# Moving the split activations to the right end of on-chip memory, and starting every large tile at a multiple of 64 bytes

## The chip, the core and the metric

The kernel runs on one NeuronCore of a Trainium2 chip. TensorE (PE) does the matrix products, VectorE (DVE), ScalarE (ACT) and GpSimd (POOL) the elementwise work, SyncE (SP) issues most transfers. All of them work on SBUF, a memory of 128 partitions; a tile is a range of byte addresses that is the same in every partition, and this case is about these addresses. The metric is the device time of one execution in microseconds (us), the median of several runs: 1369.34 us before the change.

## What is computed

Two transformer blocks on 256 tokens of 1024 features, all in fp32. The first has a projection, two attentions, gates and a MLP; the second has a gated mixing branch, a dilated attention, and PEER, a layer that picks 16 of 16384 experts per head:

```
h2 = rms_norm(x);  x = x + rms_norm(square(relu(h2 @ w_up)) @ w_down)
...
e, g = top-16 of the scores of xb @ w_query       # per token and head
act = gelu(sum_d xb[t,d] * expert_u[e,d])         # (t, h, k)
out = sum (g * act)[t,h,k] * expert_v[e,:]
```

The kernel does PEER densely: it multiplies the tokens by all of `expert_u` (16384 x 1024), weighs the result by a table that is zero but for the chosen experts, and multiplies by all of `expert_v`. These two products are 128 MB of weights and most of the time.

## The kernel before, in words

**Three products for one.** Each fp32 operand is split into a high and a low part of the type fp32r (`h` and `l`), and `mm3` (L164 to L167) issues three matmuls: high by high, high by low, low by high. Weights come by DMA into a `raw` tile of 128 x 1024 (4096 bytes per partition); ACT copies the high part to `wh` (L115), DVE or POOL subtracts to get `wl` (L121). The split activations are the tiles `hh` and `hl` (8192 bytes each: two token blocks, eight slices of 128 x 128), made by `parts()`.

**Which operand moves.** In `matmul(p, x, y)` the operand `x` is loaded into the array ahead of the matmul (a LDWEIGHTS of 128 columns, in the row PEld of the profile), and `y` streams through it. In `stations` (gate, w_up, w_query, expert_u) a weight slice is loaded and the activations stream, 256 columns in two runs of 512 bytes; in the trace these are `mid<-hh,wh`, `mid<-hl,wh`, `mid<-hh,wl`. In `project`, `rows_product`, `down` and `v_units` an activation slice is loaded and 512 columns of weights stream (`acc<-wh,ah` and the like).

**Stages and slots.** The order of all instructions on every engine is fixed when the program is built. The weights go round through slots: four pairs of the pool `ring` (always), four of the pool `wkx` (from the branch products until the routing), and in the MLP two more of the pool `wkm`, which lies on the right side. In the MLP the slots take turns as wkx, ring, wkx, ring, wkx, ring, wkx, ring, wkm, wkm; a `w_up` unit and a `w_down` unit, which alternate, take two slots each. So one w_up unit runs its first 24 matmuls on a wkx slot and its next 24 on a ring slot, and every fifth unit lies on the two wkm slots.

**Expert stages.** `expert_u` is 64 units of 48 matmuls, all on ring slots, with the activations `hh`, `hl` of the pool `hp`. During the first 32 units DVE does the routing (top-16 searches) beside the splits. During the last 32 it builds the table: for each token two tiles `m` (L1019, L1020), which PE multiplies (four matmuls `acc<-m,m` per pair of tokens, between each 12 matmuls of expert_u), then multiplies the result into `acts`. `expert_v` is 64 units of 24 matmuls of 512 columns: ring slots stream over the split `acts`, tiles `ah` and `al`.

**Addresses.** A pool takes its place when it is opened, at the left end of what is free, or at the right end where it is opened with `side="right"`; each of its tiles follows the one before it. `hp` is opened after `const`, `ring` and `small`, and so lies just right of them. The begin of the tiles that matter (bytes in a partition; every slice of 128 columns is 512 bytes, so all slices of a tile share the remainder):

| tile | begin before | mod 64 | mod 256 | begin after | mod 64 | mod 256 |
|---|---|---|---|---|---|---|
| ring: wh (first of 4) | 36128 | 32 | 32 | 37888 | 0 | 0 |
| ring: wl (first of 4) | 52512 | 32 | 32 | 54272 | 0 | 0 |
| hp: hh, hl | 70176, 78368 | 32 | 32 | 212928, 221120 | 0 | 192 |
| wkx: wh, wl (first) | 123008, 139392 | 0 | 128 | 107136, 123520 | 0 | 128 |
| MLP hh, hl (right side) | 161760, 169952 | 32 | 224 | 145344, 153536 | 0 | 192 |
| MLP wkm: wh (first of 2) | 206816 | 32 | 224 | 190400 | 0 | 192 |
| MLP mfh (first of 5) | 186336 | 32 | 224 | 169920 | 0 | 192 |
| expert_v: ah, al (first) | 152096, 156192 | 32 | 32 | 136192, 140288 | 0 | 0 |

Of the kernel before, what the change touches and what calls it, by code (L numbers as in the profile page):

```python
# [9 lines left out]
F32 = mybir.dt.float32  # L10
# [9 lines left out]
P = 128  # L20
# [10 lines left out]
HALF = 32  # L31
WBUFS = 4
RBUFS = 4


C_CAUS = 0
# [3 lines left out]
C_I50 = C_FREQ + 24  # L40
# [35 lines left out]
def block_kernel(ctx: ExitStack, tc: tile.TileContext, a, out, dbg=None):  # L76
    nc = tc.nc
    vec, act, pe, pool = nc.vector, nc.scalar, nc.tensor, nc.gpsimd

    const = ctx.enter_context(tc.tile_pool(name="const", bufs=1))  # L80
    ring = ctx.enter_context(tc.tile_pool(name="ring", bufs=1))
    small = ctx.enter_context(tc.tile_pool(name="small", bufs=4))
    hp = ctx.enter_context(tc.tile_pool(name="hp", bufs=1))
    ps = ctx.enter_context(tc.tile_pool(name="ps", bufs=1, space=PSUM))
    dram = ctx.enter_context(tc.tile_pool(name="dram", bufs=1, space=DRAM))
    xres = dram.tile([P, TB, D], F32, name="xres")
# [6 lines left out]

    cycle, raws, last_split = [ring] * WBUFS, [ring] * RBUFS, [None]
    count, turn_raw = [0, 0], [0]
# [151 lines left out]
    def project(*args, **kw):  # L247
        for _ in projecting(*args, **kw):
            pass
# [155 lines left out]
    xp = p1.enter_context(tc.tile_pool(name="xp", bufs=1))  # L405
# [78 lines left out]

    whole = [(1024, 1024)] * 2
    project(hh, hl, KB, [(f"w_in_n{W1_BLOCKS[0][0]}", 0, [(768, 768)] * 2, 384, emit_cq)])
    cst = xp.tile([P, C_I50], F32, name="cst")
    nc.sync.dma_start(out=cst, in_=a["consts"][:, :C_I50])
    tok = const.tile([P, C_N - C_I50], F32, name="tok")
    pool.dma_start(out=tok, in_=a["consts"][:, C_I50:])  # L490
    i50, i128 = tok[:, :NCAND], tok[:, NCAND:]
# [460 lines left out]
    cycle[:] = [ring] * WBUFS  # L952
    raws[:] = [ring] * RBUFS
    b1.close()
# [211 lines left out]
```

## Time and profile before

| | us |
|---|---|
| median of three runs | 1369.34 (1367.41 to 1370.09) |
| the profiled execution | 1366.17 |
| its span in the trace | 1364.4 |
| PE busy | 1320.8 (97%) |
| DVE busy | 982.0 (72%) |
| ACT busy | 667.1 (49%) |
| mean granted clock of TensorE | 0.993 of full speed |

The trace records when each instruction ran. Matmuls are pipelined, so the duration of one (0.28 us for 256 columns) overlaps the next; what one costs is the distance from its start to the start of the next. It is read here from the chain of waits (time of a stretch over its count of matmuls) or from the timeline (first and last start of a run of equal matmuls). The granted clock is 1.00 (the 2.4 GHz level) in all stretches that are compared.

### The profile page before, as it was taken

To read this page: it belongs to the slowest core of one execution; us is meant where nothing else is said; L and a number is where in the kernel's file an instruction comes from. 1 tells how busy PE (TensorE), PEld (TensorE's weight loads), DVE (VectorE), ACT (ScalarE), POOL (GpSimd) and SP (SyncE) were. 2 spreads that over 40 slices of the span, in tenths; PEclk is the share of its full clock that TensorE was granted. 3 is DMA by queue.
4 is the path that set the end of the run, shared out by engine and by line. 5 is a ranking of instruction groups with operands and counts; after the bars stand their busy time and mean duration, and the time that the engine had idled before them with its cause. 6 is when DMAs were issued, how large, how long until landed. Compare 5 with 4: busy or idle time off the path is not lost.

```text
span 1364.4 us, 22115 instructions
## 1 busy us (share of the span) xinstructions
PE 1320.8 (97%) x8324; PEld 1178.1 (86%) x8324; DVE 982.0 (72%) x2255; ACT 667.1 (49%) x1018; POOL 198.0 (15%) x103
## 2 busy tenths in 40 slices
PE   6999898999998999999999999999999999999997
PEld 5788896799986677999999999999978888888886
DVE  6666678555568795799994799999975555555555
ACT  5576545444444655355454444443435444544443
POOL 2221224322235336200000000000000000000001
PEclk9999999999999999999999999999999999999999
DMA  7453464666645425356666544444456666666662
GB/s 282 159 182 113 145 214 142 209 188 187 191 136 187 127 76 190 103 177 191 177 190 181 166 140 140 140 140 140 138 182 192 197 189 197 192 194 189 197 194 86
DMA packets 64187, 230.61 MB, mean 169 GB/s; under 512 B 7280, under 2 KB 7696, under 8 KB 63952
## 3 DMA queue, kind: packets, MB, share of 16 engines
q1 hardware_dynamic: 61632, 221.03, 52.5%
q0 software_dynamic: 1728, 6.07, 1.2%
q10 hardware_dynamic: 720, 2.10, 0.4%
q8 instruction: 65, 1.06, 0.3%
q14 instruction: 42, 0.34, 0.1%
HBM read 227.07 MB, written 2.10 MB: 168 GB/s over the span
## 4 chain that ended last, share of the span: by engine, by line
PE 90%; DVE 6%; ACT 2%; DMA 1%; issue 1%; SPq 0%; ACTq 0%; DVEq 0%
PE acc L135 52%; PE mid L135 35%; DVE wl L121 2%; PE tps L145 2%; DMA x<-in_x_dram 1%; ACT wh L115 1%; PE tps L135 1%; DVE x L244 0%; DVE ny L234 0%; DVE at_s L340 0%; ACT ny L206 0%; DVE rope_t L311 0%; DMA raw<-in_w_branch_dram 0%; DVE hl L174 0%; DVE at_s L332 0%
## 5 line engine op out<-in xcount | busy, mean ns | idle before, releaser
L115 ACT ACTIVATE wh<-raw 128x1024 fp32r<-128x1024 f32 (+2 forms) x422 | 439.2, 1047 | 421.7 <-PE mid L135 238.4
L121 DVE TENSOR_TENSOR wl<-raw,wh 128x1024 fp32r<-128x1024 f32 (+1 forms) x350 | 447.7, 1281 | 216.0 <-ACT wh L115 215.4
L135 PE MATMUL mid<-hh,wh 128*128 128x256 f32 x1280 | 372.1, 291 | 0.0
L135 PE MATMUL mid<-hh,wl 128*128 128x256 f32 x1280 | 361.2, 282 | 0.0
L135 PE MATMUL mid<-hl,wh 128*128 128x256 f32 x1280 | 361.0, 282 | 0.0
L135 PEld LDWEIGHTS mid<-hl,wh 128*128 128x128 f32 x1280 | 244.5, 191 | 0.4
L135 PEld LDWEIGHTS mid<-hh,wh 128*128 128x128 f32 x1280 | 244.1, 191 | 0.4
L135 PEld LDWEIGHTS mid<-hh,wl 128*128 128x128 f32 x1280 | 243.9, 191 | 0.0
L121 POOL TENSOR_TENSOR wl<-raw,wh 128x1024 fp32r<-128x1024 f32 (+3 forms) x72 | 176.3, 2458 | 340.4 <-ACT wh L115 297.3
L135 PE MATMUL acc<-wh,ah 128*128 128x512 f32 x512 | 200.0, 391 | 2.9 <-ACT ah L173 2.9
L135 PE MATMUL acc<-wl,ah 128*128 128x512 f32 x512 | 199.9, 390 | 0.0
L135 PE MATMUL acc<-wh,al 128*128 128x512 f32 x512 | 199.8, 390 | 0.0
L135 PE MATMUL acc<-wh,hh 128*128 128x512 f32 (+2 forms) x288 | 116.1, 403 | 1.1 <-ACT hh L173 0.9
L135 PEld LDWEIGHTS acc<-wh,ah 128*128 128x128 f32 x512 | 96.4, 188 | 23.2 <-ACT ah L173 3.1
L135 PEld LDWEIGHTS acc<-wh,al 128*128 128x128 f32 x512 | 96.6, 189 | 20.6 <-DVE al L174 0.4
L135 PEld LDWEIGHTS acc<-wl,ah 128*128 128x128 f32 x512 | 96.6, 189 | 19.9
L135 PE MATMUL acc<-wl,hh 128*128 128x512 f32 (+2 forms) x288 | 113.0, 392 | 0.6 <-POOL wl L121 0.3
L135 PE MATMUL acc<-wh,hl 128*128 128x512 f32 (+2 forms) x288 | 112.6, 391 | 0.4 <-DVE hl L174 0.2
L1020 DVE TENSOR_SCALAR m<-tok,key,gwt 128x128 f32<-128x128 f32 x256 | 89.2, 349 | 0.0
L173 ACT ACTIVATE ah<-acts 128x512 fp32r<-128x512 f32 x64 | 40.3, 632 | 91.8 <-PE acc L135 89.2
L174 DVE TENSOR_TENSOR al<-acts,ah 128x512 fp32r<-128x512 f32 x64 | 44.3, 693 | 52.8 <-ACT ah L173 52.8
L1019 DVE TENSOR_SCALAR m<-tok,key 128x128 f32<-128x128 f32 x256 | 73.7, 289 | 6.5 <-PE acc L135 5.6
(259 smaller groups left out, 1703.2 us busy)
## 6 DMA issues: line engine op xcount, KB each, us to landing
raw<-in_expert_u_dram SPq DMA_DIRECT2D x128, 512.0 KB, 3.7
raw<-in_expert_v_dram SPq DMA_DIRECT2D x128, 512.0 KB, 4.5
raw<-in_w_down_dram SPq DMA_DIRECT2D x32, 512.0 KB, 4.4
raw<-in_w_up_dram SPq DMA_DIRECT2D x24, 512.0 KB, 4.7
raw<-in_w_in_dram SPq DMA_DIRECT2D x20, 512.0 KB, 4.7
raw<-in_w_gate_dram SPq DMA_DIRECT2D x16, 512.0 KB, 4.0
raw<-in_w_out_dram SPq DMA_DIRECT2D x16, 512.0 KB, 4.7
raw<-in_w_in_n_dram SPq DMA_DIRECT2D x12, 512.0 KB, 4.6
```

Of the source, the lines that this page charges most:

```text
L115: i = act.activation(h[:, :n], raw[:, :n], AF.Copy)
L121: last_split[0] = eng.tensor_tensor(l[:, :n], raw[:, :n], h[:, :n].bitcast(F32), op=OP.subtract)
L135: in_line(pe.matmul(p, x, y, start=start, stop=stop))
L145: in_line(pe.transpose(out, src, ident))
L173: turned_[0] = act.activation(h, p, AF.Copy)
L174: vec.tensor_tensor(l, p, h.bitcast(F32), op=OP.subtract)
L1019: vec.tensor_scalar(m2, i128, key2[:, t:t + 1], None, op0=OP.is_equal)
L1020: vec.tensor_scalar(m1, i128, key1[:, t:t + 1], gwt[:, t:t + 1], op0=OP.is_equal, op1=OP.mult)
```

## The change

Two tiles that nothing uses, `gap` (480 bytes) and `gapr` (32 bytes), push the pools behind them. `small` is opened ahead of `ring` instead of behind it. `hp` is opened on the right side, where it lies at the end of SBUF and pushes every right-side pool of the stages by 16416 bytes to the left; the left-side pools behind it (`xp`, `wk1`, `wkx`, `pk` with `acts`, `ab`, `pv`) come to lie some 15900 bytes lower. `cst` is made 928 columns wide instead of 920, of which 920 are loaded as before, so that the pools behind `xp` also start at a multiple of 64 bytes.

No instruction is added, removed or moved: every engine has the same instructions in the same order, with the same waits on the same semaphores, before and after; the SBUF addresses are all that differs.

```
     const = ctx.enter_context(tc.tile_pool(name="const", bufs=1))
+    small = ctx.enter_context(tc.tile_pool(name="small", bufs=4))
+
+    gap = ctx.enter_context(tc.tile_pool(name="gap", bufs=1))
+    gap.tile([P, GAP], F32, name="gap")
     ring = ctx.enter_context(tc.tile_pool(name="ring", bufs=1))
-    small = ctx.enter_context(tc.tile_pool(name="small", bufs=4))
-    hp = ctx.enter_context(tc.tile_pool(name="hp", bufs=1))
+    gapr = ctx.enter_context(tc.tile_pool(name="gapr", bufs=1, side="right"))
+    gapr.tile([P, 8], F32, name="gapr")
+    hp = ctx.enter_context(tc.tile_pool(name="hp", bufs=1, side="right"))
...
-    cst = xp.tile([P, C_I50], F32, name="cst")
-    nc.sync.dma_start(out=cst, in_=a["consts"][:, :C_I50])
+    cst = xp.tile([P, 928], F32, name="cst")
+    nc.sync.dma_start(out=cst[:, :C_I50], in_=a["consts"][:, :C_I50])
```

(`GAP = 120` stands with the other constants.)

## Rows read from the trace of the kernel before

**Rows 1.** The page: busy time by engine, and the chain that ended last.

```profile
PE 1320.8 (97%) x8324; PEld 1178.1 (86%) x8324; DVE 982.0 (72%) x2255; ACT 667.1 (49%) x1018; POOL 198.0 (15%) x103
...
PE acc L135 52%; PE mid L135 35%; DVE wl L121 2%; PE tps L145 2%; DMA x<-in_x_dram 1%; ACT wh L115 1%; PE tps L135 1%; DVE x L244 0%; DVE ny L234 0%; DVE at_s L340 0%; ACT ny L206 0%; DVE rope_t L311 0%; DMA raw<-in_w_branch_dram 0%; DVE hl L174 0%; DVE at_s L332 0%
```

**Rows 2.** The chain in order of time: start us, us, what; expert_u, then expert_v.

```profile
581.77 97.91 PE mid L135 x816
679.68 0.33 PE tps L145 x3
680.01 69.11 PE mid L135 x576
...
749.45 15.83 PE mid L135 x132
...
840.93 1.43 PE mid L135 x12
842.37 0.45 PE acc L135 x4
...
1005.16 347.64 PE acc L135 x1524
```

**Rows 3.** PE's timeline, a w_up unit: wkx slot from 285.69, ring slot from 288.56.

```profile
285.69 0.28 PE L135 MATMUL mid<-hh,wh 128*128 128x256 f32 x1
...
288.56 0.28 PE L135 MATMUL mid<-hh,wh 128*128 128x256 f32 x1
...
291.28 0.40 PE L135 MATMUL acc<-wh,mfh 128*128 128x512 f32 x1
```

**Rows 4.** PE's timeline, the w_up unit on the two wkm slots.

```profile
308.00 0.28 PE L135 MATMUL mid<-hh,wh 128*128 128x256 f32 x1
...
313.76 0.39 PE L135 MATMUL acc<-wh,mfh 128*128 128x512 f32 x1
```

**Rows 5.** PE's timeline, the ring slot of an earlier w_up unit.

```profile
266.15 0.28 PE L135 MATMUL mid<-hh,wh 128*128 128x256 f32 x1
...
268.98 0.39 PE L135 MATMUL acc<-wh,mfh 128*128 128x512 f32 x1
```

**Rows 6.** PE's timeline, w_down: wkm (282.96 on), wkx (291.52 on), ring (294.10 on).

```profile
282.96 0.39 PE L135 MATMUL acc<-wh,mfh 128*128 128x512 f32 x1
...
285.45 0.40 PE L135 MATMUL acc<-wh,mfl 128*128 128x512 f32 x1
...
291.52 0.40 PE L135 MATMUL acc<-wl,mfh 128*128 128x512 f32 x1
...
293.86 0.40 PE L135 MATMUL acc<-wh,mfl 128*128 128x512 f32 x1
...
294.10 0.39 PE L135 MATMUL acc<-wh,mfh 128*128 128x512 f32 x1
...
296.62 0.39 PE L135 MATMUL acc<-wh,mfl 128*128 128x512 f32 x1
```

**Rows 7.** Stretches: length, busy PE, PEld, DVE, ACT, POOL; PEclk, DMA share, GB/s.

```profile
87.00:160.00 73.00, 71.66 (x563) 64.50 (x561) 44.99 (x143) 48.15 (x123) 14.32 (x6) 1.00 0.38 122
...
540.00:585.00 45.00, 45.00 (x362) 43.88 (x361) 33.27 (x184) 21.50 (x31) 15.06 (x7) 1.00 0.42 125
585.00:640.00 55.00, 55.00 (x461) 55.00 (x460) 55.00 (x198) 27.58 (x32) 0.00 (x0) 1.00 0.59 180
...
765.00:850.00 85.00, 85.00 (x726) 85.00 (x725) 80.17 (x257) 37.99 (x66) 0.00 (x0) 1.00 0.46 141
850.00:950.00 100.00, 100.00 (x853) 100.00 (x853) 98.36 (x306) 41.90 (x81) 0.00 (x0) 1.00 0.47 142
950.00:1004.00 54.00, 51.89 (x440) 51.51 (x439) 54.00 (x159) 20.50 (x42) 1.14 (x2) 1.00 0.45 139
1004.00:1355.00 351.00, 349.84 (x1535) 289.29 (x1536) 201.33 (x205) 167.63 (x195) 3.14 (x3) 1.00 0.61 186
```

**Rows 8.** Waits from 581 to 1004 us: who for whom, us, times, longest.

```profile
DVE m L1019 <- PE acc L135: 5.6, 22, 0.4
```

More of the change, by code (lines that the diff above doesn't have):

```diff
@@ L33 @@
 RBUFS = 4
+GAP = 120
 C_CAUS = 0
```

## The prediction, made before the changed kernel ran

> **What bounds the kernel now.** I read the page first. PE is busy 97% of the span, and the chain that ended last is PE for 87% by two kinds of matmul, `acc` and `mid` [rows 1]. So time is won or lost by what a matmul costs, or where PE waits. The chain in order of time gives that cost by stage [rows 2]: in the first half of expert_u 816 + 576 + 132 = 1524 matmuls of 256 columns take 97.91 + 69.11 + 15.83 = 182.85 us, 120.0 ns each, without a gap. In expert_v 1524 matmuls of 512 columns take 347.64 us, 228.1 ns each. The difference is 108 ns for 256 columns, 0.42 ns a column, which is one column per cycle at the granted 2.4 GHz. So 256 columns are 106.7 ns, and about 13 ns of each matmul are something else, at either width. No view names it. Over the 3072 matmuls of expert_u it is 41 us, over the 1536 of expert_v 20 us or a little more.
>
> Next I asked whether this extra time is the same everywhere, since the change only moves tiles. It is not. In the MLP the same 256-column matmul runs in the same stage on three kinds of slot. A unit on the two wkm slots takes 313.76 - 308.00 = 5.76 us for 48, 120.0 ns each [rows 4]. Another unit takes 2.87 us for 24 on a wkx slot, 119.6 ns each, and then 291.28 - 288.56 = 2.72 us for 24 on a ring slot, 113.3 ns each [rows 3]. Shapes, order and clock are equal; only the weights' addresses differ. The ring half of an earlier unit reads otherwise: 2.83 us for 24, 117.9 ns [rows 5].
>
> The table of addresses has two properties that go with 113.3. First, the distance: the activations begin 192 bytes (mod 256) past the ring weights there, against 0 for wkm and 0 for expert_u, both at 120.0. Second, the place: the activations lie right and the ring left there, while in expert_u both lie below 87000 and in the wkm unit both on the right. The trace can't part these two. For expert_u it need not: after the change hh and hl are 192 bytes (mod 256) past the ring, and at the right end. Both properties say that expert_u becomes what the ring half of the w_up unit is.
>
> **A rule that speaks against it.** The w_up unit reads 119.6 and 113.3 ns by the slot alone [rows 3]. The Trainium skill, page "TensorE: Matmul & The Clock Gate", section "Step-by-step: what each phase is for", says that PE has two independent read ports into SBUF, so that loading the next weights takes no bandwidth from the running matmul. By it no address should matter and the time stays 1369; the rows contradict it here, and I keep it as the rival of no change below, with the chance that the rows leave it. Its section "Back-to-back issue gap" puts a lone gap at N/2.4 + 2.5 ns, an estimate of 109 ns for 256 columns and 216 ns for 512: the rows are 11 and 12 ns above, and the ring half of w_up 4.
>
> **The change part by part.** It adds and removes no work, so every term is a count of matmuls by a difference per matmul.
>
> *expert_u, first half.* 1524 matmuls x (120.0 - 113.3) = 10.2 us. What could be late next is DVE: it is busy 55.0 of 55 us from 585 to 640 [rows 7], where routing and splits overlap, though PE never waits for it there. At the new pace these 55 us become 52. I charge 0.4, between 0 and the 3 us that it costs if the cover is all used: 9.8 us.
>
> *expert_u, second half.* A pair of tokens is 12 matmuls in 1.43 us and four table products in 0.45 [rows 2], 128 times. PE alone would win 12 x 6.7 = 80 ns a pair, 10.3 us. But DVE is busy 80.2 of 85, 98.4 of 100 and 54.0 of 54 us there [rows 7]: 232.5 of 239, and waits for PE only 5.6 us in all [rows 8]. DVE's work does not shrink, so the stretch can't lose much more than the 6.5 us. I take 6.0; from below it is 4, if DVE can't start its part earlier.
>
> *w_query and gates.* 192 matmuls of w_query lie in 540 to 585, where PE is busy 45.0 of 45 [rows 7]: 192 x 6, 1.1 us. The gate units (384 matmuls, same tiles) fill the waits of an attention; PE is busy 71.7 of 73 [rows 7]. 384 x 6.7 = 2.6 at most, nothing if the softmax chain ends last; I take half, 1.3.
>
> *w_up and branches.* Distances of ring (192) and wkm (0) stay, so 113.3 and 120.0 stay. On wkx slots the distance goes from 96 to 64, a value of which no row of 256 columns tells: 240 matmuls between 119.6 and 113.3, 0 to 1.5 us; 0.6. The branch products are 192 matmuls with the same new distances: 0.3.
>
> *512 columns with activations loaded.* Projections, w_out, w_up's first blocks, w_down, w_in of the second block. There the w_down rows are 226.4 ns at distance 0, 229.1 at 64 (from the ring) and 234 on wkx slots [rows 6]. The projections leave distance 0 for 64 (+2.7 ns, some 400 matmuls, +1 us), the wkx slots leave their old distances, all worth 5 ns or less on a few hundred. I take 0, with 2 us either way.
>
> *expert_v.* Ring and ah, al began at the same remainder and still do (32 and 32 before, 0 and 0 after), and distance 0 is also what the wkm rows at 226.4 have, with other remainders. So nothing changes: 0. That all are now at multiples of 64 is what no row of this shape shows. Its bounds: the extra 13 to 15 ns can go altogether, 1536 x 14.8 = -22.7 us, or half of it as in w_up, 1536 x 6.7 = -10.3; on the other side it can become the 234 of the wkx slots, +9 us. I stay with 0, since the nearest rows have the same distance.
>
> *The price per matmul in expert_u itself* has bounds too: no lower than the 110 ns at which three transposes of 128 columns follow each other (0.33 us for three [rows 2]), each with a weight load of the same size; no higher than the 120.0 of now, but for the case in which aligned weights are slow, below. The two row values between are 113.3 and 117.9.
>
> Transfers, ACT and DVE work keep their order; a faster expert_u asks for its 1 MB per unit in 5.44 instead of 5.76 us, which is the rate at which expert_v already runs (24 x 228 ns = 5.47 us for 1 MB, DMA share 0.61 [rows 7]).
>
> **The sum.** 9.8 + 6.0 + 1.1 + 1.3 + 0.6 + 0.3 = 19.1 us. The profiled execution took 1366.17 us, so it would be 1347.1; the median of the runs lies 3.2 us above that execution: 1350.
>
> **Rivals.**
>
> *1. The slower rhythm.* The same ring slots gave 117.9 ns once [rows 5], so the extra time hangs on how the streams fall into step. If expert_u falls into that one: 1524 x 2.1 = 3.2, second half 3.2, the rest 1.5; 7.9 us, 1361. For it: the one unit. Against it: the ring half of rows 3 came behind a wkx slot as well and runs at 113.3; and in expert_u every unit follows one of the same distance, so that a faster rhythm, once found, is not disturbed.
>
> *2. Alignment pays as well.* A tile at a multiple of 64 bytes saves something in each matmul, expert_v included: the main sum and half the extra of expert_v, 19.1 + 10.3, 1340; with all of it 1327. Against it: the wkx slots are the one place of now whose weights begin at a multiple of 64, and they are not faster: 119.6 against 113.3, and 234 against 229 [rows 3, 6]. There the partner is not aligned, though.
>
> *3. Nothing.* By the two-port rule named above, or because the 113.3 has another reason in the MLP (the unit's neighbours, POOL): all terms 0, 1369. Against it: the two halves of one unit differ, and the wkm unit has the same neighbours.
>
> *4. Aligned weights are the slow ones.* Read the wkx rows the other way round: a ring at a multiple of 64 behaves like wkx. Then expert_v goes to 234 ns, 1536 x 5.9 = +9.1 us, expert_u stays near 119.6 (-1), the projections on ring slots add 5 ns on 400 (+2): 1379. It decides if ring matmuls of expert_v read above 232. Against it: the wkx distances (96, 160) are as good a reason.
>
> **Chances.** The forecast 0.56; slower rhythm 0.12; alignment pays too 0.17; nothing 0.08; slow alignment 0.07. The range: the forecast's own is 1344 to 1355 (the second half's 4 to 6.5, the gates 0 to 2.6, 2 us of the projections). It reaches to rival 1 above and to the half of rival 2 below: 1336 to 1363. A measurement of this kernel can tell 0.2% (2.7 us) from no change. Faster by more than that: 0.56 + 0.12 + 0.17 = 0.85, less 0.01 for a rival 1 that loses its 7.9 us in the other stages: 0.84. Within 0.2%: the 0.08 of rival 3 and that 0.01, 0.09. Slower: the 0.07 of rival 4.
>
> **What would show it.** Right: the chain's long pieces of expert_u at 113 ns each (the first 32 units end some 10 us sooner); in the second half DVE busy all the time and PE with small gaps before the table products; expert_v at 227 to 228. Wrong: expert_u at 118 or 120, or at 110; expert_v off its 228 by more than 2 ns; wkm units of w_up off 120, since their distance stays.

## The result and the profile after

The changed kernel takes 1354.72 us (median of 4 runs, 1353.66 to 1357.89) against 1368.38 us for the kernel before (4 runs, 1367.00 to 1370.09): a ratio of 0.9903, 95% interval 0.9882 to 0.9925. The gain is 13.7 us where 19.1 was forecast; the time lies 4.7 us above the 1350.0 predicted and inside the range.

The profiled execution of after is the slowest of its four runs, 1357.89 us (span 1356.1), while that of before lay 2.2 us under its group's median. So the two traces differ by 8.3 us only. The page after, to be laid beside [rows 1]:

```profile
PE 1310.0 (97%) x8324; PEld 1166.8 (86%) x8324; DVE 979.8 (72%) x2255; ACT 667.1 (49%) x1018; POOL 197.8 (15%) x103
...
PE 80%; DVE 13%; issue 2%; ACT 2%; DMA 1%; SPq 0%; POOL 0%; ACTq 0%; DVEq 0%
PE acc L141 52%; PE mid L141 27%; DVE wl L127 4%; PE tps L151 2%; ACT wh L121 1%; DMA x<-in_x_dram 1%; DVE eq L902 1%; DVE ef L904 1%; PE tps L141 1%; DVE x L250 1%; DVE eq L899 1%; DVE at_s L346 1%; DVE tk_w L821 0%; DVE ny L240 0%; ACT ny L212 0%
```

PE does the same 8324 matmuls in 10.8 us less. `mid`, the 256-column stages, went from 35% of the chain to 27%, and DVE stands there with 13%: a sign that DVE's splits now arrive just in time. Line numbers of after are those of before plus 6. The chain in order of time (start us, us, what) beside [rows 2]:

```profile
582.59 2.75 PE mid L141 x24
...
687.41 56.57 PE mid L141 x478
...
744.31 14.98 PE mid L141 x132
759.73 1.42 PE mid L141 x12
...
840.83 1.42 PE mid L141 x12
842.25 0.45 PE acc L141 x4
842.70 1.38 PE mid L141 x12
844.08 0.44 PE acc L141 x4
...
996.10 348.39 PE acc L141 x1524
```

In the trace of before, the first run of 12 behind table products is

```profile
765.73 1.43 PE mid L135 x12
```

The first half of expert_u, from its first matmul to this run, went from 765.73 - 581.77 = 183.96 us to 759.73 - 582.59 = 177.14. It has two speeds; a steady price per matmul is called a rhythm below. Up to 687 us the matmuls follow each other at 113.3 ns (14.98 / 132 at the end reads the same), and from 687.41 on 478 of them take 56.57 us, 118 ns each, the slower rhythm of [rows 5]. In the second half, runs of 12 take 1.42 and 1.38 us by turns, where all took 1.43 before; it went from 239.43 to 236.37 us. The stretches, as in [rows 7]:

```profile
585.00:640.00 55.00, 55.00 (x487) 55.00 (x487) 55.00 (x205) 28.85 (x34) 0.00 (x0) 1.00 0.61 182
765.00:850.00 85.00, 85.00 (x740) 85.00 (x739) 81.97 (x265) 39.57 (x69) 0.00 (x0) 1.00 0.49 144
850.00:950.00 100.00, 100.00 (x870) 100.00 (x869) 99.73 (x309) 42.21 (x82) 0.00 (x0) 1.00 0.48 143
```

From 585 to 640 PE gets 487 matmuls done instead of 461, with DVE busy all the time. The waits of PE from 581 to 1004 us (who for whom, us, times, longest) hold one for a split, of the kind that before did not have:

```profile
PE acc L141 <- ACT ah L179: 2.9, 1, 2.9
PE acc L141 <- DVE m L1026: 1.4, 2, 1.1
PE mid L141 <- DVE wl L127: 0.8, 1, 0.8
```

The w_up units show all three distances in one stage (PE's timeline; the starts of a unit and of the next stage):

```profile
263.84 0.28 PE L141 MATMUL mid<-hh,wh 128*128 128x256 f32 x1
...
269.50 0.40 PE L141 MATMUL acc<-wh,mfh 128*128 128x512 f32 x1
...
308.40 0.28 PE L141 MATMUL mid<-hh,wh 128*128 128x256 f32 x1
...
314.16 0.40 PE L141 MATMUL acc<-wh,mfh 128*128 128x512 f32 x1
```

A unit on a wkx slot (distance now 64) and a ring slot (192) takes 5.66 us for 48, 117.9 ns, or 5.56 with the ring half at 114: four units of each kind, as the ring half had both rhythms before in [rows 3, 5]. The wkm unit (distance 0) stays at 5.76 us, 120.0, as in [rows 4].

### The profile page after: what moved, and what is told of

It is laid out like the page before. It is cut to its first block, busy times and chain, and to the rows that moved or that the text cites. A ratio compares the mean times of both kernels' runs of the same rounds, so it can differ in the third digit from the quotient of the medians.

```text
span 1356.1 us, 22115 instructions
## 1 busy us (share of the span) xinstructions
PE 1310.0 (97%) x8324; PEld 1166.8 (86%) x8324; DVE 979.8 (72%) x2255; ACT 667.1 (49%) x1018; POOL 197.8 (15%) x103
## 4 chain that ended last, share of the span: by engine, by line
PE 80%; DVE 13%; issue 2%; ACT 2%; DMA 1%; SPq 0%; POOL 0%; ACTq 0%; DVEq 0%
PE acc L141 52%; PE mid L141 27%; DVE wl L127 4%; PE tps L151 2%; ACT wh L121 1%; DMA x<-in_x_dram 1%; DVE eq L902 1%; DVE ef L904 1%; PE tps L141 1%; DVE x L250 1%; DVE eq L899 1%; DVE at_s L346 1%; DVE tk_w L821 0%; DVE ny L240 0%; ACT ny L212 0%
## 5 line engine op out<-in xcount | busy, mean ns | idle before, releaser
L141 PE MATMUL mid<-hh,wh 128*128 128x256 f32 x1280 | 367.8, 287 | 0.0
L141 PE MATMUL mid<-hh,wl 128*128 128x256 f32 x1280 | 356.4, 278 | 0.8 <-DVE wl L127 0.8
L141 PE MATMUL mid<-hl,wh 128*128 128x256 f32 x1280 | 356.6, 279 | 0.0
L141 PEld LDWEIGHTS mid<-hh,wh 128*128 128x128 f32 x1280 | 241.1, 188 | 0.4
L141 PEld LDWEIGHTS mid<-hh,wl 128*128 128x128 f32 x1280 | 240.4, 188 | 1.0 <-DVE wl L127 1.0
L141 PE MATMUL acc<-wh,hh 128*128 128x512 f32 (+2 forms) x288 | 117.2, 407 | 1.3 <-ACT hh L179 1.2
L1026 DVE TENSOR_SCALAR m<-tok,key,gwt 128x128 f32<-128x128 f32 x256 | 94.7, 372 | 0.0
L1025 DVE TENSOR_SCALAR m<-tok,key 128x128 f32<-128x128 f32 x256 | 79.4, 311 | 3.8 <-PE acc L141 3.0
```

Source lines behind the costliest of these rows:

```text
L141: in_line(pe.matmul(p, x, y, start=start, stop=stop))
L1025: vec.tensor_scalar(m2, i128, key2[:, t:t + 1], None, op0=OP.is_equal)
L1026: vec.tensor_scalar(m1, i128, key1[:, t:t + 1], gwt[:, t:t + 1], op0=OP.is_equal, op1=OP.mult)
```

## The experiments

Theory 1 says that the distance between the begin of the streaming operand and that of the loaded block (modulo 256 bytes) sets the extra time; its rivals are the place at the right end (theory 2) and the multiple of 64 (theory 3). Theory 4 came from the trace of after: DVE is the next limit in expert_u. In the table below, times of stages are from the first matmul of a stage to that of the next, found by the matmul's number in the program; ratios are against runs of the kernel before on the same chip (its medians there lay between 1368.07 and 1369.00), with 95% intervals. The stage times are those of one profiled run each.

| kernel | median us | ratio | expert_u 1st half | 2nd half | expert_v |
|---|---|---|---|---|---|
| before | 1368.38 | | 184.08 | 239.35 | 349.95 |
| after | 1354.72 | 0.9903 (0.9882 to 0.9925) | 177.25 | 236.30 | 350.71 |
| place alone | 1368.77 | 0.9997 (0.9988 to 1.0005) | 184.08 | 239.38 | 349.99 |
| distance alone | 1354.85 | 0.9895 (0.9880 to 0.9910) | 175.50 | 236.28 | 349.52 |
| after, distance 0 | 1367.08 | 0.9991 (0.9982 to 0.9999) | 184.08 | 239.38 | 349.96 |
| after, routing step 2.6 | 1353.21 | 0.9888 (0.9874 to 0.9903) | 175.94 | 236.29 | 349.56 |
| after, routing step 2.4 | 1353.84 | 0.9887 (0.9868 to 0.9905) | 174.05 | 236.29 | 350.60 |
| after, distance 112 | 1356.61 | 0.9911 (0.9894 to 0.9928) | 175.30 | 238.26 | 350.59 |
| distance 112, step 2.4 | 1354.48 | 0.9897 (0.9879 to 0.9916) | 174.20 | 238.26 | 349.57 |
| step 2.4, half of m2 left out | 1349.94 | 0.9865 (0.9847 to 0.9884) | 176.38 | 233.53 | 348.47 |
| step 2.4, four tokens at a time | 1350.46 | 0.9872 (0.9852 to 0.9892) | 174.06 | 234.98 | 350.91 |

### Place alone, distance alone, distance taken back

To the kernel before:

```
-    hp = ctx.enter_context(tc.tile_pool(name="hp", bufs=1))
+    gapa = ctx.enter_context(tc.tile_pool(name="gapa", bufs=1, side="right"))
+    gapa.tile([P, 48], F32, name="gapa")
+    hp = ctx.enter_context(tc.tile_pool(name="hp", bufs=1, side="right"))
+    gapb = ctx.enter_context(tc.tile_pool(name="gapb", bufs=1, side="right"))
+    gapb.tile([P, 16], F32, name="gapb")
```

> The kernel before with one edit: the activations hh and hl go to the right end of SBUF, behind a tile of 192 bytes and ahead of one of 64. Their begin is 32 modulo 256, so the distance from a loaded activation block to a ring half that streams over it stays 0 modulo 256 as in the kernel before, and no large tile begins at a multiple of 64. Theory 1 (the distance modulo 256 sets the 6.7 ns): the 256-column matmuls stay at 120.0 ns, expert_u's first half takes about 184 us, time 1368. Theory 2 (the place at the right end sets it): 113.3 ns there, about 177 us, time 1355. Theory 3 (the multiple of 64 sets it): 120.0 ns, 1368.

To the kernel before, all on the left side:

```
+    gapa = ctx.enter_context(tc.tile_pool(name="gapa", bufs=1))
+    gapa.tile([P, 48], F32, name="gapa")
     hp = ctx.enter_context(tc.tile_pool(name="hp", bufs=1))
+    gapb = ctx.enter_context(tc.tile_pool(name="gapb", bufs=1))
+    gapb.tile([P, 16], F32, name="gapb")
```

> The kernel before with one edit: hh and hl stay at the left, with a tile of 192 bytes ahead and one of 64 behind. They begin at 224 modulo 256, the ring at 32, so the distance is 192 modulo 256 as in the changed kernel; no large tile begins at a multiple of 64. Theory 1 (distance): 113.3 ns in expert_u until VectorE's lead is used up near 690 us, first half about 177 us, time 1355. Theory 2 (place): 120.0 ns, 184 us, 1368. Theory 3 (multiple of 64): 120.0 ns, 184 us, 1368.

To the changed kernel:

```
-    gapr = ctx.enter_context(tc.tile_pool(name="gapr", bufs=1, side="right"))
-    gapr.tile([P, 8], F32, name="gapr")
+    gapa = ctx.enter_context(tc.tile_pool(name="gapa", bufs=1, side="right"))
+    gapa.tile([P, 56], F32, name="gapa")
     hp = ctx.enter_context(tc.tile_pool(name="hp", bufs=1, side="right"))
+    gapb = ctx.enter_context(tc.tile_pool(name="gapb", bufs=1, side="right"))
+    gapb.tile([P, 16], F32, name="gapb")
```

> The changed kernel with one edit: hh and hl, still at the right end and at a multiple of 64, are moved by 192 bytes so that they begin at 0 modulo 256 like the ring, distance 0. Theory 1 (distance): 120.0 ns again, first half of expert_u about 184 us, time 1368. Theories 2 and 3 (place, multiple of 64): 113.3 ns stays, 177 us, 1355.

The chain of waits reads, for place alone:

```profile
584.53 97.91 PE mid L139 x816
```

for distance alone:

```profile
582.50 40.83 PE mid L139 x360
...
687.11 54.46 PE mid L139 x478
...
741.90 15.55 PE mid L139 x132
```

and for the changed kernel with distance 0:

```profile
582.54 97.91 PE mid L143 x816
```

97.91 us for 816 is 120.0 ns, to the hundredth what [rows 2] have; 40.83 for 360 is 113.4. The tile of 192 bytes ahead of `hp` gives all that the change gives. The move to the other end alone gives nothing (0.9997); everything in the change but the distance of `hp` gives some 2.5 us at most (1367.08; the ratio lies between 0.9982 and 0.9999). Theory 1 holds, theories 2 and 3 fall.

### The distance by itself

Small programs, only matmuls of the kernel's shapes with chosen offsets, one run of each:

```
for place in (left, right):
    for base in (0, 32):
        for d in range(0, 256, 32):    # begin of hh, hl = base + d; of x, y = base
            4 x (4 fp32 products, 12 matmuls of 256 columns), then 48 matmuls
```

> A small program by itself, which computes none of the reference: matmuls of 256 and 512 columns in the shapes of the kernel (a 128x128 block loaded, the other operand streaming, in triples of high and low parts), for every distance between the begin of the streaming operand and that of the loaded one from 0 to 224 modulo 256 in steps of 32, with the activations at the left or at the right end of SBUF, and with the loaded or streaming tile at 0 or 32 modulo 64. Theory 1: the mean interval depends on the distance alone (120.0 ns at 0, 113.3 at 192, for 256 columns), and is the same for both places and both bases; the other distances are not known. Theory 2: left and right differ by 6.7 ns. Theory 3: base 0 and base 32 differ by 6.7 ns. For 512 columns with activations loaded theory 1 gives 226.7 ns at 0.

The chain of this program; a piece of 60 is the last 12 and the 48, a piece of 36 is of 512 columns:

```profile
18.42 7.20 PE acc L42 x60
...
97.38 7.08 PE acc L42 x60
...
202.59 6.82 PE acc L42 x60
...
228.65 7.20 PE acc L42 x60
...
412.82 6.82 PE acc L42 x60
433.24 8.19 PE acc L42 x36
...
485.94 8.40 PE acc L42 x36
```

In order: left, base 0, distance 0 (120.0 ns); the same at 192 (118); left, base 32, distance 192 (113.7 with the first of the piece); right, base 0, distance 0 (120.0); right, base 32, distance 192 (113.7); then 512 columns, base 0, at 0 (227) and 192 (233). In the long runs left and right, and base 0 and 32, agree within 0.1 ns at each distance but 192. There both rhythms occur: each setting has four runs, and with base 0 the second and the fourth read 117.8 at either end, while all others, and all with base 32, read 113.3 to 113.5. In the kernel, base 32 (distance alone) has both rhythms too: 113.4 ns at 582.50 and 15.55 / 132 = 117.8 at 741.90 above.

The finer steps:

> As the program before it (it computes none of the reference), with the distance in steps of 8 bytes, at the left end alone, for 256 columns (runs of 12 matmuls behind two fp32 pairs, three times, and one of 48) and for 512 columns (24 matmuls). The coarse table had 120.0, 116.7, 117.8, 120.0, 120.0, 118.6, 113.3 or 117.8, and 118.3 ns at 0, 32, ... 224. If the slower rhythm of distance 192 belongs to the edge of a flat region, a distance near it (168 to 216) holds 113.3 ns in all its runs; if the chance of either rhythm lies in how a run starts, the neighbours show both as well. For 512 columns a distance below 226.7 ns is possible but nothing speaks for it.

| distance | 0 | 16 | 32 | 48 | 64 | 80 | 96 | 112 |
|---|---|---|---|---|---|---|---|---|
| ns, 256 columns | 120.0 | 116.7 | 116.7 | 118.4 | 117.8 | 118.3 | 119.9 | 113.3 |

| distance | 128 | 144 | 160 | 176 | 192 | 208 | 224 | 240 |
|---|---|---|---|---|---|---|---|---|
| ns, 256 columns | 120.0 | 118.7 | 118.8 | 119.3 | 113.4, 117.9 | 119.2 | 118.3 | 117.2 |

(Runs of 48; for 192 both values that its four runs had; the first run of 112 read 117.8 as well.) Odd multiples of 8 bytes take 120.0 to 126.6. For 512 columns 0 is the best of the 32 distances, 227.2 ns, 64 has 229.4, and all others 231 to 236. So 120.0 was one of the worst places for 256 columns on the 16-byte grid, and the one good one for 512.

> The same sort of program (it computes none of the reference) at 256 columns, with the offsets of the high half hh, the low half hl of the streaming operand and of the low block y against the high block x chosen apart, each 0, 64, 128 or 192 bytes. If a stream is disturbed by the load that runs beside it, that of the next matmul (hh beside x, hl beside y, hh beside the next x), the time goes by the two distances hh-x and hl-y, and hh-y alone changes nothing: with both at 192 the time is 113.3 or 117.8 ns whatever y's own offset. If a stream is disturbed by its own loaded block, it goes by hh-x, hl-x and hh-y.

```
for dy in (0, 64, 128, 192):        # begin of y against x
    for dh in (0, 64, 128, 192):    # begin of hh against x
        for dl in (0, 64, 128, 192):    # begin of hl against x
            2 x (4 fp32 products, 12 matmuls), 36 matmuls
```

Neither theory of which pair matters came out (hh-x is the begin of hh less that of x, modulo 256). With hh-x and hl-y at 192, moving y changed the time (113.3 and 117.8 with y at 0; 117.8 to 120.9 with y elsewhere), against the first. The second names three distances, which fix a setting, so it can't fall as a whole; but a distance carries no price of its own: hh-x and hl-x at 192 with hh-y at 64 gave 113.7 in both runs, though all at 64 take 117.8. But for the first run, at the lower clock level (213 ns), all 64 settings lie between 113.3 and 121.8 ns. Which accesses meet is open.

### Why the gain is smaller than the distance promises

Theory 4. The routing work that DVE takes on after each unit of expert_u's first half is a step in us, `route(3.0)`; a smaller step spreads it. To the changed kernel:

```
-        route(3.0)
+        route(2.6)
```

> The changed kernel with the planner's step of VectorE's routing work in expert_u set to 2.6 instead of 3.0 us, so that this work is spread over more of expert_u's first half. Theory 4 (VectorE's routing work uses up its lead on the weight splits; one wait of 0.8 us near 688 us then throws TensorE into the 117.7 ns rhythm until 743): no wait and no 117.7 ns stretch, first half about 174 us instead of 177.1, time 1349 to 1353. Rival (the slower rhythm comes without any wait, from the chip): a stretch of 117.7 ns stays and the time is 1355. Rival (the VectorE work only moves to the second half): first half 174, second half longer by as much, time 1355.

The wait near 688 us is gone, and yet 117.7 ns came, at another place: from 640.8 us to the three transposes at 691.35, where it went back to 113.3 (59.86 / 528 is 113.4).

```profile
580.58 110.77 PE mid L141 x960
691.35 0.33 PE tps L151 x3
691.68 59.86 PE mid L141 x528
```

So theory 4 as I had put it is not the whole, and the first rival is not it either: something started the stretch. The same with `route(2.4)`:

> The changed kernel with the routing step at 2.4 us instead of 3.0, distance 192. If the slower rhythm in the first half begins where VectorE's lead is used up (near 640 and 688 us), it is gone, and the first half takes 173 to 174 us, time 1351 to 1353. If it begins at the pauses of about 0.3 us that every kernel has there (near 691 and 745 us), a stretch of 117.7 ns stays and the half takes 174 to 178.

No stretch of 117.7 is left, in the chain:

```profile
582.32 119.75 PE mid L141 x1056
702.07 0.33 PE tps L151 x3
702.40 48.99 PE mid L141 x432
```

113.4 ns each, 174.05 us for the half, 10.0 less than before. The time of the whole, 1353.84, is above the 1351 to 1353 expected, and its interval overlaps that of after. Another run warns against crediting the routing with the faster rhythm. The kernel below with half of `m2` left out has the same program up to the second half, and its chain reads

```profile
581.02 122.08 PE mid L141 x1056
703.11 0.33 PE tps L151 x3
703.44 48.98 PE mid L141 x432
```

with 117.8 ns from 641.1 to 702.6 and 176.38 us for the half. Same instructions, same addresses, two outcomes. Where they part can be seen in the loads of weights (PEld's timeline), first of the run that kept 113.3, then of the one that did not:

```profile
641.90 0.19 PEld L141 LDWEIGHTS mid<-hh,wh 128*128 128x128 f32 x1
642.02 0.19 PEld L141 LDWEIGHTS mid<-hl,wh 128*128 128x128 f32 x1
642.16 0.19 PEld L141 LDWEIGHTS mid<-hh,wl 128*128 128x128 f32 x1
```

```profile
640.61 0.19 PEld L141 LDWEIGHTS mid<-hh,wh 128*128 128x128 f32 x1
640.72 0.19 PEld L141 LDWEIGHTS mid<-hl,wh 128*128 128x128 f32 x1
640.88 0.19 PEld L141 LDWEIGHTS mid<-hh,wl 128*128 128x128 f32 x1
```

Loads start every 0.11 us; the first block of `wl` of this unit starts 25 ns late in the one and 52 ns late in the other. DVE's lead, the time from the end of a split to the first matmul that uses it, is some 4 us at 588 us; at this unit it is down to 0.1 us. Eight kernels have distance 192 or 112: after, distance alone, steps 2.6 and 2.4, both with 112, and the two below. In seven of them this load is late, by 25, 37, 38, 40, 52, 78 and 91 ns. Those with 37 and 52 went on at 117.8; the other five fell back to 113.3 within a dozen matmuls. In the eighth, distance alone, the lead is 0.35 us here, and nothing is late or changes.

Distance alone also shows that a longer wait need not bring the slower rhythm. At 687 us PE waits 0.6 us for a split there, as it waits 0.8 us in after; yet the 478 matmuls behind it take 54.46 us, 113.9 ns each, where those of after take 118. The expectation had the slower rhythm begin there; it began only behind the three transposes that follow at 741 us (15.55 / 132 is 117.8). With step 2.6, three such transposes had ended it. So in these first halves a rhythm lasts until PE is disturbed, by a load some tens of ns late, a wait or three transposes. Which rhythm follows goes neither by the length nor by the kind of the disturbance; what decides it is open.

112 instead of 192 was tried for a distance that holds the faster rhythm (hh and hl as views that begin 112 bytes past a multiple of 256, everything else unchanged modulo 256; the lines that do the latter are left out):

```
+    def padded(name, dt):
+        return hp.tile([P, 2112], dt, name=name)[:, 36:2084]
...
```

> The changed kernel with the distance alone at 112 instead of 192, routing step 3.0 as in the changed kernel. If 112 holds 113.3 ns also through the second half's units of 12 matmuls: second half 230 to 234 us instead of 236.3, first half 174 to 177 (the wait near 688 us stays), time 1347 to 1352. If 112 is no better than 192: 1353 to 1356.

With the routing step of 2.4 as well:

> The changed kernel with hh and hl begun 112 bytes past a multiple of 256 (distance 112 to the ring halves instead of 192), and the step of the routing work in expert_u at 2.4 us instead of 3.0. If 112 holds 113.3 ns more steadily than 192 (three of four runs in the fine table, two of four for 192) and VectorE's lead no longer runs out: first half of expert_u 173 to 174 us, second half 230 to 234 us (VectorE has 99.7% there, so not below 230), time 1344 to 1350. If the rhythm is drawn anew at every pause whatever the distance: first half 174 to 178, second half 236, time 1352 to 1355.

The first half is no worse (174.20 and 175.30 us), but in the second all runs of 12 take 1.42 us, and it takes 2 us more than with 192. The hope of the expectations failed: three of four runs at 113.3 in the small program did not carry over, and 1356.61 us lies above both times expected of distance 112 alone. The chain of distance 112 alone:

```profile
765.94 1.42 PE mid L141 x12
...
767.81 1.42 PE mid L141 x12
```

What holds the second half at 236.3 us? Two edits on the kernel with step 2.4:

```
-            m2 = ab.tile([P, P], F32, name="m2", bufs=6)
-            vec.tensor_scalar(m2, i128, key2[:, t:t + 1], None, op0=OP.is_equal)
+            if t % 2 == 0:
+                m2 = ab.tile([P, P], F32, name="m2", bufs=6)
+                vec.tensor_scalar(m2, i128, key2[:, t:t + 1], None, op0=OP.is_equal)
```

> The changed kernel with routing step 2.4 (second half of expert_u 236.3 us) and with half of VectorE's one-hot tiles m2 left out in the second half: of two tokens the second uses the tile of the first, so the mixing weights of every odd token are wrong. VectorE loses 128 x 0.28 = 36 us of some 233. If VectorE holds the second half back, it shrinks to what TensorE alone needs at 113.3 ns, about 229 us, and the units of 12 matmuls take 1.38 us each. If TensorE's rhythm holds it (113 and 118 ns by turns in the units), the units stay as they are and only the wait of about 1.4 us at the end goes: 234.5 to 236 us, time 1352 to 1354.

```profile
765.00:850.00 85.00, 85.00 (x740) 85.00 (x739) 73.18 (x219) 39.55 (x70) 0.00 (x0) 1.00 0.46 143
850.00:950.00 100.00, 100.00 (x870) 100.00 (x869) 91.95 (x260) 44.09 (x81) 0.00 (x0) 1.00 0.46 143
```

DVE now has 12 and 8 us to spare in these stretches, and PE does the same 740 and 870 matmuls to the last one. So DVE did not set the pace there; PE's rhythm did. By matmul number, all that is won, 2.8 us, lies in the last 6 us of the stage, where the wait of 1.4 us for `m` is gone and the granted clock of the stretch from 975 to 1004 stays at 1.00 (0.88 with step 2.4 alone). The half, 233.53 us, came out below the 234.5 to 236 expected, which left the clock out.

The second edit:

```
-            if t % 2:
+            if t % 4 == 3:
                 yield
+                yield
```

> The changed kernel with routing step 2.4 and the table products of the second half taken four tokens at every second turn instead of two at every turn: TensorE's runs of 256-column matmuls there are 24 long instead of 12, with 64 interruptions instead of 128. If every interruption draws the rhythm anew and costs something by itself, the second half gets shorter by the cost of 64 interruptions, a few us: 231 to 235, and a run is either all 113.3 or all 117.7 ns. If the bursts make TensorE wait for VectorE's one-hot tiles, it gets longer than 236.3 and the trace shows waits for m.

```profile
765.58 2.74 PE mid L141 x24
768.32 0.89 PE acc L141 x8
769.21 2.83 PE mid L141 x24
```

Runs of 24 in 2.74 and 2.83 us, 114 and 118 ns, strictly by turns again, as the runs of 12 are in after: where the interruptions are regular, the rhythm that follows repeats too. The second half is 1.3 us shorter, 0.6 of it up to 17 us before its end, so the 64 interruptions that are gone cost little by themselves. The kernel is the fastest that computes everything, 1350.46 us; its interval overlaps those of after and of step 2.4, so that it is better than the changed kernel is likely and not shown.

## Why the prediction was right, and where it was off

*The reading of expert_u by the ring half of w_up* was right, and the experiment that changes the distance alone shows which of the two properties counts, which the trace of before could not separate: distance, not place. The price of 113.3 ns was right to the tenth, for the faster rhythm. The rival of no change falls: 192 bytes are worth 1368.79 - 1354.85 = 13.9 us. The Trainium skill (page "TensorE: Matmul & The Clock Gate", section "Step-by-step: what each phase is for") says that loading the next weights takes no read bandwidth from the running matmul. What the forecast drew from that, that no address should matter, does not hold here: 120.0 and 113.3 ns differ by two addresses alone. Whether it is the load that slows the running matmul, no run here shows.

*expert_u, first half: 9.8 forecast, 6.8 in the profiled run.* The count and the price hold: 10.0 us with step 2.4. The step that failed is in rival 1, "a faster rhythm, once found, is not disturbed". DVE's cover was used up, as the bound of 0 to 3 us allowed, but not as a wait of that length: in the profiled run PE waited 0.8 us once, and 40 ns at 641 us, and most of the cost is the slower rhythm behind the wait, 478 x 4.4 = 2.1 us. Over the profiled runs with distance 192 the half's gain is 6.8 to 10.0.

*expert_u, second half: 6.0 forecast, 3.1 measured.* The mechanism named was wrong here. I let DVE cap the gain at 6.5; DVE's 99.73 of 100 us looked like it. The term that failed is another, the 80 ns that PE alone was to win per pair of tokens. A pair took 1.43 + 0.45 = 1.88 us before; in after it takes 1.42 + 0.45 = 1.87 in the slower rhythm and 1.38 + 0.44 = 1.82 in the faster. By the starts of the matmuls that is 17 and 57 ns won, by turns, not 80. The slower rhythm in every other run costs 64 x 40 ns, 2.6 of the 10.3 us; 2.9 more are missing since even a faster run begins with matmuls of 116 to 120 ns behind the table products. What is left was there: by matmul number, 4.6 us were won up to 6 us before the stage's end, and 1.5 lost behind that, in the wait for `m` and at the lower clock. Freeing DVE changed nothing until that end, so DVE capped the end alone. "DVE busy all the time" came true and proved nothing: DVE waited for PE's results 3.0 us in 14 waits, and from the end of a split to its first use there were 8.4 to 8.9 us between 770 and 920 us. The small gaps that PE was to show before the table products did not come. With DVE freed the gain is 239.35 - 233.53 = 5.8, near the 6.0 by luck: it is made up of other parts. (The counts were a little off: one unit of expert_u runs ahead of the stretch that the forecast counts, and the second half has 125 runs of 12, not 128.)

*Small terms.* w_query 0.8 (1.1 forecast), gates 1.1 (1.3), w_up 0.6 (0.6; the wkm unit stayed at 120.0), branches -0.3 (0.3). expert_v stayed at 227 ns from start to start, as forecast; its distance stayed 0. Its stage is 0.8 us longer in the profiled run of after and 0.4 shorter in that of distance alone. That goes with the granted clock around its start, behind PE's wait of 2.9 us for `ah`: from 975 to 1004 us it is 0.88 in after, 0.94 in distance alone, and 1.00 with half of `m2` left out, which has the shortest stage, 348.47.

*The sum against the runs.* The profiled pair gives 8.3 us, the medians 13.7. The profiled run of before was a lucky one: its mean granted clock is 0.993, while 21 of 23 later runs of before have 0.987 to 0.990, and the profiled run of after 0.988. One stretch shows it, before and then after:

```profile
405.00:440.00 35.00, 30.87 (x133) 23.89 (x133) 31.45 (x53) 16.59 (x21) 20.43 (x8) 0.95 0.50 157
```

```profile
405.00:440.00 35.00, 30.55 (x126) 23.30 (x126) 28.73 (x48) 16.56 (x22) 19.29 (x8) 0.90 0.47 152
```

The same matmuls, w_down's last part, take 34.73 us before and 36.48 after, 1.75 more, with a granted clock of 0.95 and 0.90. Place alone and distance 0, at the slow price of everything else, have 36.36 and 36.33 there, at 0.90. Two more stretches (155 to 180 and 220 to 245 us) have 0.93 before and 0.86 after, and after takes 1.2 us longer in each; that this is the clock alone is not shown, since distance 0, also at 0.86, is only 0.2 and 0.7 us longer there. These three stretches and the 0.8 of expert_v make up 4.9 us, nearly all that lies between 8.3 and 13.7. So the medians are the better figure. The forecast, 19.1, exceeds them by 5.4 us: 2.9 of the second half, 0 to 3 of the first by the rhythm that follows a disturbance, about 1 in the small terms; what is left over is not assigned. The time came out at the upper edge of the forecast's own 1344 to 1355.

*The rivals.* Alignment pays too: no, expert_v did not move, and distance 0 with aligned tiles is slow again, within 0.2% of before. Aligned weights slow: no, ring matmuls of expert_v read 227 ns, not above 232. The slower rhythm as a whole: it took a part of each half, not all.

## What to carry to other kernels

Where a profile shows the same matmul at two prices in one stage, compare the begin addresses of the operand that streams and of the block that is loaded, modulo 256: one unused tile of 192 bytes was worth 1% here, and the best distance differs by width (0 for 512 columns; 192 or 112 for 256, where 0 is slow in every run). A busy share near 100% on a second engine does not make it the limit: look at whether it runs ahead of the first, or take work off it. And when a stage shows two rhythms, look for the first disturbance before the change of pace, and read several traces before crediting an edit with the better one.

## What the runs showed of the hardware that was not expected

A streaming matmul's extra time depends on the distance modulo 256 between two SBUF addresses in steps of 16 bytes, from 113.3 to 120.0 ns at 256 columns, and odd multiples of 8 bytes cost up to 126.6. At distances 192 and 112 two steady rhythms exist, 113.3 and 117.8 ns. A weight load that came 37 or 52 ns late was followed by the slower one for 50 and 61 us, until three transposes of 0.33 us (at 691 and 703 us), while delays of 25, 38, 40, 78 and 91 ns were not. In the run of distance alone three such transposes began the slower rhythm instead.
